# A wait of every GpSimd operation for the VectorE operation before it in the plan, in a fully planned decoder block

## The chip, the cores and the metric

The kernel runs on one core of one Trainium2 chip. The metric is device time in microseconds (us) from the start to the end of one execution; the median of several runs counts. The engines are named as in the profile: PE is TensorE (matrix products), PEld its weight loads, ACT is ScalarE, DVE is VectorE, POOL is GpSimd, SP is the engine whose queue issues the DMA transfers. SBUF is the memory that all of them read and write, PSUM the one into which TensorE writes.

## What is computed

One layer of a decoder with three parallel token mixers, for 1024 tokens of 1024 channels in float32. Cut to what matters:

```
h = rmsnorm(x);  proj = h @ w_in              # 1024 x 9744 columns
y_ssd = ssd_mixer(conv(z, xBC, dt))           # width-4 conv, chunked scan, 16 heads
y_lru = rglru_mixer(conv(lru_x), gelu gate)   # width-4 conv, linear recurrence
y_ret = retention_mixer(rotary(q, k), v, g)   # 4 heads, chunks of 128
merged = sum_k sigmoid(gate_k) * (y_k @ w_branch[k])
x = x + merged @ w_o
a, u = split(rmsnorm(x) @ ffn_w_in)           # 3072 columns each
x = x + (gelu(conv3(a)) * u) @ ffn_w_out
return rmsnorm(x)
```

## The kernel before

Activations are held transposed: channels on the 128 partitions, tokens along the row, in tiles of 128 x 512 (half of the tokens, called half 0 and 1). Every large product is done as a "quad" of two column blocks by two token halves, with seven partial products in place of eight (products named A11, S1 to S4 on the weight's side and B11, T1 to T4 on the activation's side; sums and differences of blocks are formed on VectorE at L342, L353 and L407). Each operand is split into a high part, rounded on ScalarE (L260), and a low part, the difference, formed on VectorE or GpSimd (L336 for activations, L420 for weights); three matmuls (L444 to L446) make one product. Results are combined out of PSUM on VectorE (L426). Between the quads run the small stages: convolutions (L504 to L517: a GpSimd or VectorE memset or a copy of three halo columns, one ScalarE pass and two or three VectorE steps at L514), the scan (L780 to L878), retention (L981 to L1046), the recurrence (L893 to L953), gates and sums (L1133 to L1228).

Nothing is issued directly. Every step is recorded as an `Op` in a `Plan` with the engines that may run it, an estimated duration, a priority, and its dependences. `Plan.schedule` then plays all engines against a clock and gives each Op an engine, a start and its buffers; `run` issues the Ops in the order of their planned start, with tc.manual_schedule(), so each engine's program order is the plan's. The framework places semaphore waits for the data dependences between engines, and no others.

The plan has a notion of a shared port. An Op is marked when it can run on VectorE and reads nothing from PSUM (L74):

```python
o.lock = "DVE" in engs and len({id(b) for b in r if b.tag in PSUMS}) == 0
```

and in `schedule` a GpSimd Op and a marked VectorE Op are never planned at the same time (L177, and L224 to L225):

```python
ok = not (port > t and (e == "POOL" or (e == "DVE" and o.lock))) and fits(o)
...
if e == "POOL" or (e == "DVE" and o.lock):
    port = t + dur
```

On the chip nothing holds the two engines to this: a GpSimd operation starts when its own data and buffers are there. Simple elementwise steps are recorded with `vec(..., pool=True)`, which lets the plan choose between VectorE and GpSimd; `gps` records GpSimd alone. The functions that record ScalarE and TensorE steps, and four helpers of the softplus at the start, issue their instructions inside a function that returns nothing; the others return the instruction.

Of the kernel before, what the change touches and what calls it, by code (L numbers as in the profile page):

```python
# [240 lines left out]
class K:  # L241
# [1072 lines left out]
    def run(self, gl):  # L1314
        tc, nc = self.tc, self.nc
        with tc.tile_pool(name="small", bufs=1) as small, \
                tc.tile_pool(name="big", bufs=1) as pool, \
                tc.tile_pool(name="psum", bufs=1, space=PSUM) as psum, \
                tc.tile_pool(name="dram", bufs=1, space=DRAM) as dpool:
            self.small, self.dpool = small, dpool  # L1320
            self.load_consts()
            self.record(gl)
            slots = dict(SLOTS)
            for key in self.OPS:
                for p in range(4):
                    for s in "hl":
                        slots[f"{key}{s}{p}"] = 1
            ops = self.pl.schedule(slots)
            eng = {"PE": nc.tensor, "ACT": nc.scalar, "DVE": nc.vector, "POOL": nc.gpsimd, "DMA": nc.sync}
            with tc.manual_schedule():  # L1330
                for op in ops:
                    for b in op.alloc:
                        pl = psum if b.tag in PSUMS else pool
                        b.t = pl.tile(b.shape, b.dt, name=b.name, tag=f"{b.tag}_{b.slot}")
                    op.fn(eng[op.eng])


def pairs():
# [97 lines left out]
```

## Time and profile before

| | |
|---|---|
| median of 3 runs | 2113.42 us (2112.43 to 2116.41) |
| the profiled execution | 2117.82 us, its span 2116.1 us |
| mean granted TensorE clock | 0.991 |
| busy: TensorE | 2061.2 us, 97% of the span |
| busy: VectorE | 1683.1 us, 80%, 2635 instructions |
| busy: ScalarE | 1146.4 us, 54% |
| busy: GpSimd | 652.0 us, 31%, 514 instructions |

Busy time is the time in which an instruction of the engine is under way, standing for something else included. A busy share is a mean over stages. In the timelines a row is start, duration, engine, line, operation, what it writes and reads, shape, how many such instructions are merged in the row; in brackets the idle time of the engine just before it, and what ended it. VectorE's instructions follow one another with a small overlap, so that a row may start up to 0.09 us before the one ahead of it ends.

### The profile page before, as it was taken

The page shows a single profiled execution, that of the slowest core. Times are in us where ns is not written, and L with a number is a line of the kernel's source. Part 1 is how long each engine was busy: PE and PEld are TensorE (multiplying, and loading weights), DVE is VectorE, ACT ScalarE, POOL GpSimd, SP SyncE. Part 2 cuts the span into 40 slices and gives each one's busy share as a digit, 9 for nine tenths or more (in the row PEclk, how much of TensorE's full clock was granted, in tenths as well). Part 3 has the DMA queues.
Part 4 walks back from the last instruction along what each step waited for, and adds up shares of the span by engine and source line. Part 5 has one row for each costly group of instructions (what it writes and reads, how often), then busy time and mean ns, then how long its engine had stood idle before and what let it go on. Part 6 is the DMA issues. An engine that isn't in the chain of part 4 may idle for free.

```text
span 2116.1 us, 27857 instructions
## 1 busy us (share of the span) xinstructions
PE 2061.2 (97%) x9390; PEld 1656.1 (78%) x9390; DVE 1683.1 (80%) x2635; ACT 1146.4 (54%) x1927; POOL 652.0 (31%) x514
## 2 busy tenths in 40 slices
PE   8999999999999999999999999989999999999997
PEld 4788888678888888888877877768888888887886
DVE  7979999987754557667889989897777777899887
ACT  6645465445766679999644335454434444544442
POOL 3111134432212111212466545442211221244441
PEclk9999999999999999999999999989999999999998
DMA  4333335534354544445678856713222222276764
GB/s 167 130 114 123 113 110 164 167 138 138 122 168 157 162 146 159 149 154 198 198 239 278 268 188 202 245 55 110 99 101 80 90 75 81 89 251 213 258 214 164
DMA packets 148032, 332.04 MB, mean 157 GB/s; under 512 B 16432, under 2 KB 17200, under 8 KB 147888
## 3 DMA queue, kind: packets, MB, share of 16 engines
q1 hardware_dynamic: 147888, 330.26, 47.3%
q8 instruction: 74, 1.21, 0.2%
q14 instruction: 70, 0.57, 0.1%
HBM read 235.82 MB, written 94.37 MB: 156 GB/s over the span
## 4 chain that ended last, share of the span: by engine, by line
PE 69%; DVE 6%; DMA 3%; issue 1%; ACT 1%; POOL 0%; SPq 0%; DVEq 0%; ACTq 0%; POOLq 0%
PE y_ff L444 3%; PE y_ff L446 3%; PE y_ff L445 3%; PE z_ff L446 2%; PE x_ff L445 2%; PE z_ff L444 2%; PE x_ff L444 2%; PE z_ff L445 2%; PE x_ff L446 2%; PE y_gt L446 2%; PE y_gt L444 2%; PE y_gt L445 2%; PE y_fo L444 1%; PE y_fo L446 1%; PE y_fo L445 1%; PE y_br L444 1%
## 5 line engine op out<-in xcount | busy, mean ns | idle before, releaser
L260 ACT ACT_TABLE_LOAD x102 | 130.9, 1283 | 1.9
L426 DVE TENSOR_TENSOR e_ff<-e_ff,y_ff 128x512 f32<-128x512 f32 x72 | 49.5, 687 | 60.8 <-PE y_ff L446 58.6
L1205 POOL TENSOR_TENSOR cv_fa<-cv_fa,e_ff 128x512 f32<-128x512 f32 x26 | 34.6, 1331 | 72.4 <-DVE e_ff L426 63.6
L260 ACT ACTIVATE cv_fa<-cv_fa 128x512 f32<-128x512 f32 x48 | 30.4, 633 | 44.5 <-DVE cv_fa L514 42.4
L426 DVE TENSOR_TENSOR e_gt<-e_gt,y_gt 128x512 f32<-128x512 f32 x36 | 24.6, 684 | 24.6 <-PE y_gt L446 24.6
L514 DVE SCALAR_TENSOR_TENSOR cv_fa<-o_fa,consts,cv_fa 128x512 f32<-128x512 f32 x48 | 41.3, 860 | 2.0
L1228 POOL TENSOR_TENSOR e_fo<-e_fo,xl 128x512 f32<-128x512 f32 x23 | 30.2, 1312 | 38.1 <-DVE e_fo L426 36.1
L260 ACT ACTIVATE mt<-ps_a,acs 128x128 f32<-128x128 f32 x128 | 39.1, 363 | 0.4
L514 DVE SCALAR_TENSOR_TENSOR cv_fa<-e_ff,consts,cv_fa 128x512 f32<-128x512 f32 x48 | 35.9, 748 | 1.3 <-ACT cv_fa L260 0.5
L846 POOL TENSOR_TENSOR mt<-mt,cbt 128x512 f32<-128x512 f32 x15 | 20.6, 1374 | 47.0 <-ACT mt L260 40.7
L426 DVE TENSOR_TENSOR e_ff<-e_ff,z_ff 128x512 f32<-128x512 f32 x48 | 32.9, 686 | 2.5 <-PE z_ff L446 0.9
L426 DVE TENSOR_TENSOR e_fo<-e_fo,y_fo 128x512 f32<-128x512 f32 x36 | 24.6, 684 | 9.4 <-PE y_fo L446 9.1
L514 DVE SCALAR_TENSOR_TENSOR cv_lx<-e_lx,consts,cv_lx 128x512 f32<-128x512 f32 x36 | 28.5, 821 | 0.7 <-ACT cv_lx L260 0.5
L426 DVE TENSOR_TENSOR e_br<-e_br,y_br 128x512 f32<-128x512 f32 x36 | 24.6, 683 | 5.2 <-PE y_br L446 4.9
L1139 POOL TENSOR_TENSOR e_br<-e_br,gl 128x512 f32<-128x512 f32 x17 | 23.6, 1388 | 16.6 <-DVE e_br L426 16.5
L260 ACT ACTIVATE e<-ps_a 64x512 f32<-64x512 f32 x32 | 18.9, 592 | 17.1 <-PE ps_a L834 16.9
L514 DVE SCALAR_TENSOR_TENSOR cv_xs<-e_xs,consts,cv_xs 128x512 f32<-128x512 f32 x36 | 27.7, 814 | 0.1
L925 PE MATMUL ps_l<-lxh,lwl 128*128 128x512 f32 x64 | 25.2, 394 | 0.0
L924 PE MATMUL ps_l<-lxl,lwh 128*128 128x512 f32 x64 | 25.2, 394 | 0.0
L923 PE MATMUL ps_l<-lxh,lwh 128*128 128x512 f32 x64 | 25.2, 394 | 0.0
L260 ACT ACTIVATE e_gt<-e_gt 128x512 f32<-128x512 f32 x36 | 21.8, 625 | 5.8 <-DVE e_gt L426 5.7
L868 POOL TENSOR_TENSOR xs<-xs,e 128x384 f32<-128x384 f32 (+1 forms) x10 | 13.3, 1330 | 35.1 <-DVE xs L866 28.4
(6116 smaller groups left out, 8059.4 us busy)
## 6 DMA issues: line engine op xcount, KB each, us to landing
wr_ff<-in_ffn_in_dram SPq DMA_DIRECT2D x50, 512.0 KB, 3.8
wr_fo<-in_ffn_out_dram SPq DMA_DIRECT2D x43, 512.0 KB, 4.4
wr_br<-in_w_branch_dram SPq DMA_DIRECT2D x35, 512.0 KB, 4.7
yl<-yd SPq DMA_DIRECT2D x60, 256.0 KB, 4.9
gl<-g SPq DMA_DIRECT2D x60, 256.0 KB, 4.5
wr_gt<-in_w_quads_dram SPq DMA_DIRECT2D x24, 512.0 KB, 5.0
gl<-gt SPq DMA_DIRECT2D x48, 256.0 KB, 3.7
g<-cv_fa SPq DMA_DIRECT2D x48, 256.0 KB, 2.0
```

The source lines that it names most:

```text
L260: e.activation(out(), in_(), func, **kw)
L426: q.k.vec(lambda e: e.tensor_tensor(out.t[:, O:], a.t[:, O:], ps.t, ALU.add), [a, ps], [out], prio=pr)
L444: e.matmul(ps.t, ah.t[:, c], bh.t, start=(start and m == 0), stop=False, **kw)
L445: e.matmul(ps.t, ah.t[:, c], bl.t, start=False, stop=False, **kw)
L446: e.matmul(ps.t, al.t[:, c], bh.t, start=False, stop=(m == 3), **kw)
L514: self.vec(lambda e, s=s: e.scalar_tensor_tensor(cv.t[:, O:], raw.t[:, O - s : W - s], w(taps - 1 - s), cv.t[:, O:], ALU.mult, ALU.add), [ ...
L923: e.matmul(p_.t, wh.t[:, s], h.t, start=(k == 0), stop=False)
L924: e.matmul(p_.t, wh.t[:, s], l.t, start=False, stop=False)
L925: e.matmul(p_.t, wl.t[:, s], h.t, start=False, stop=(k == 1))
L1139: self.vec(lambda e: e.tensor_tensor(out.t[:, o], ap(), g.t[:, o], ALU.mult), [buf, g], [out], pool=not ps)
L1205: self.vec(lambda e: e.tensor_tensor(a.t[:, o], a.t[:, o], u.t[:, o], ALU.mult), [a, u], [a], pool=True)
L1228: self.vec(lambda e: e.tensor_tensor(out.t[:, o], ap(), x.t[:, o], ALU.add), [buf, x], [out], pool=not ps)
```

## The change

The loop that issues the plan remembers the last VectorE instruction that came from a marked Op (`op.lock`) and returned an instruction. Each GpSimd instruction then gets a dependence on it, of the class that is kept by a semaphore, so that it does not start before that VectorE instruction has ended. The plan itself, its order, engines and buffers are as before.

```diff
             eng = {"PE": nc.tensor, "ACT": nc.scalar, "DVE": nc.vector, "POOL": nc.gpsimd, "DMA": nc.sync}
+
+            info = mybir.DependencyInfo(mybir.DependencyClass.Sync, mybir.DependencyReason.DATA)
+            holder = None
             with tc.manual_schedule():
                 for op in ops:
                     for b in op.alloc:
                         pl = psum if b.tag in PSUMS else pool
                         b.t = pl.tile(b.shape, b.dt, name=b.name, tag=f"{b.tag}_{b.slot}")
-                    op.fn(eng[op.eng])
+                    ins = op.fn(eng[op.eng])
+                    if op.eng == "DVE" and op.lock and ins is not None:
+                        holder = ins
+                    elif op.eng == "POOL" and holder is not None:
+                        tc.add_manual_dep(ins.ins, holder.ins.name, info, reason="port order")
```

## Rows read from the trace of the kernel before

**Rows 1.** The page of the profile: the engines' busy time, share and instructions, and the chain of work that ended last, its share by engine.

```profile
span 2116.1 us, 27857 instructions
...
PE 2061.2 (97%) x9390; PEld 1656.1 (78%) x9390; DVE 1683.1 (80%) x2635; ACT 1146.4 (54%) x1927; POOL 652.0 (31%) x514
...
PE 69%; DVE 6%; DMA 3%; issue 1%; ACT 1%; POOL 0%; SPq 0%; DVEq 0%; ACTq 0%; POOLq 0%
```

**Rows 2.** The view of waits, TensorE's alone: who waited for whom, us in total, times, the longest.

```profile
PE ss_fin L551 <- DVE acc_fin L571: 2.6, 1, 2.6
...
PE x_ff L445 <- POOL h2B11l L336: 1.2, 1, 1.2
...
PE ps_y L862 <- POOL mt L846: 0.6, 1, 0.6
```

**Rows 3.** The timeline around 1395 us, VectorE's and GpSimd's rows; ahead of them one unhindered row of each, at 1390 and 1391.

```profile
1390.14 0.69 DVE L342 TENSOR_TENSOR h2T<-e_wo,x 128x512 f32<-128x512 f32 x1
...
1394.48 1.29 DVE L342 TENSOR_TENSOR h2T<-e_wo,x 128x512 f32<-128x512 f32 x1
...
1395.69 1.77 DVE L342 TENSOR_TENSOR h2T<-e_wo,x 128x512 f32<-128x512 f32 x1
...
1391.45 1.28 POOL L420 TENSOR_TENSOR ff0A22l<-wr_ff,ff0A22h 128x512 fp32r<-128x512 f32 x1 [1.78 <-ACT ff0A22h L260]
...
1395.16 1.74 POOL L336 TENSOR_TENSOR h2T2l<-x,h2T2h 128x512 fp32r<-128x512 f32 x1
```

**Rows 4.** The timelines of GpSimd and VectorE: two memsets, the VectorE operation in whose time the second falls, and the step that reads its columns.

```profile
115.19 0.10 POOL L508 MEMSET o_B<- 128x3 f32 x1
...
1490.26 1.23 DVE L510 COPY e_ff<-halo 128x3 f32<-128x3 f32 x1
...
1491.37 0.10 POOL L508 MEMSET o_fa<- 128x3 f32 x1
...
1501.32 0.76 DVE L514 SCALAR_TENSOR_TENSOR cv_fa<-o_fa,consts,cv_fa 128x512 f32<-128x512 f32 x1
```

**Rows 5.** The timeline of GpSimd: the first and the last of 57 GpSimd operations with inputs that start while the VectorE operation before them in the plan runs.

```profile
42.48 1.87 POOL L336 TENSOR_TENSOR hB22l<-x,hB22h 128x512 fp32r<-128x512 f32 x1 [1.62 <-ACT hB22h L260]
...
2027.27 1.68 POOL L1228 TENSOR_TENSOR e_fo<-e_fo,xl 128x512 f32<-128x512 f32 x1 [1.23 <-DVE e_fo L426]
```

**Rows 6.** The chain of work that ended last, in order of time: start, us, what (POOLq is GpSimd's sequencer), near 1369, 1146 and 1401 us.

```profile
1369.34 0.60 DVE acc_ffn L571
...
1370.06 0.02 POOLq L1166
1370.08 1.26 POOL acc_ffn L571
...
1146.73 4.50 DMA yl<-yd
...
1401.17 0.67 DVE cv_fa L514
```

**Rows 7.** The timelines: VectorE operations that stood behind a GpSimd operation which had itself stood behind the VectorE operation before; the first (381) and the last (2024) of ten, two between, and a GpSimd row that follows the one at 1938.

```profile
381.76 1.78 DVE L1309 TENSOR_TENSOR e_qk<-e_qk,rt 128x512 f32<-128x512 f32 x1
...
389.41 1.68 DVE L846 TENSOR_TENSOR mt<-mt,cbt 128x512 f32<-128x512 f32 x1
...
1938.01 1.79 DVE L342 TENSOR_TENSOR g1T<-gl,gl 128x512 f32<-128x512 f32 x1
...
1945.16 1.74 POOL L336 TENSOR_TENSOR g1B22l<-gl,g1B22h 128x512 fp32r<-128x512 f32 x1
...
2024.81 1.79 DVE L342 TENSOR_TENSOR g2T<-gl,gl 128x512 f32<-128x512 f32 x1
```

**Rows 8.** The timelines: VectorE operations that started after a GpSimd operation which the plan has behind them; of 12, the GpSimd operation of the first (138), both operations of the last (1298), and three of VectorE's between.

```profile
138.29 1.30 POOL L420 TENSOR_TENSOR xs0A11l<-wr_xs,xs0A11h 128x512 fp32r<-128x512 f32 x1 [2.88 <-ACT xs0A11h L260]
...
438.06 1.77 DVE L407 TENSOR_TENSOR v1S<-wr_v 128x512 f32<-128x512 f32 x1
...
1141.61 1.82 DVE L342 TENSOR_TENSOR y2T<-yl,yl 128x512 f32<-128x512 f32 x1
...
1143.35 1.79 DVE L342 TENSOR_TENSOR y2T<-yl,yl 128x512 f32<-128x512 f32 x1
...
1298.24 1.75 POOL L336 TENSOR_TENSOR mgT2l<-m,mgT2h 128x512 fp32r<-128x512 f32 x1
...
1298.76 1.79 DVE L407 TENSOR_TENSOR wo0S<-wr_wo,wr_wo 128x512 f32<-128x512 f32 x1
```

**Rows 9.** The timeline of TensorE: five matmuls before which it stood, the stop in brackets.

```profile
385.95 1.16 PE L851 MATMUL ps_of<-Cm,sv 128*128 128x128 f32 x8 [1.39 <-DVE sv L825]
...
444.68 0.50 PE L444 MATMUL x_v<-hB21h,v0A12h 128*128 128x512 f32 x1 [0.80 <-ACT e_v L260]
...
1156.39 0.50 PE L444 MATMUL y_br<-y2T3h,br20S3h 128*128 128x512 f32 x1 [1.68 <-DVE e_br L426]
...
1405.03 0.51 PE L444 MATMUL z_ff<-h2T1h,ff1S1h 128*128 128x512 f32 x1 [1.20 <-ACT ff1S1h L260]
...
1950.30 0.50 PE L444 MATMUL x_fo<-g1B21h,fo11A12h 128*128 128x512 f32 x1 [2.92 <-ACT e_fo L260]
```

**Rows 10.** The timelines of GpSimd and TensorE: a GpSimd operation that starts inside a VectorE operation, and the matmuls that read its result.

```profile
331.10 1.56 POOL L846 TENSOR_TENSOR mt<-mt,cbt 128x512 f32<-128x512 f32 x1 [6.38 <-ACT mt L260]
...
332.71 0.98 PE L862 MATMUL ps_y<-mt,xdt 128*64 128x128 f32 x13 [0.65 <-POOL mt L846]
```

## The prediction

> **What bounds the kernel now.** I read the page first, for which engine is full; then TensorE's waits, for what stops that engine; then the two timelines of VectorE and GpSimd side by side, because the change touches only the order between those two; last the chain of waits, to see which of their operations lie ahead of a TensorE stop. The reader is to see that TensorE is busy for 2061.2 of the 2116.1 us span, with most of the chain that ended last on it, 6% on VectorE and 0% on GpSimd, which is busy 31% of the time [rows 1]. So no change in the order of VectorE and GpSimd can give more than the 54.9 us in which TensorE stands idle, and of those some are the first load and waits for ScalarE. The longest single wait that VectorE ends is 2.6 us, and only two waits are GpSimd's own, 1.2 and 0.6 us [rows 2].
>
> **What the two engines do to each other.** An h2T subtraction of two SBUF tiles takes 0.69 us when nothing is in its way. The one at 1395.69 takes 1.77, because the GpSimd operation that started at 1395.16 sits in the middle of it; and that GpSimd operation, issued 0.61 us before the VectorE operation ahead of it ended, takes 1.74 where an unhindered one takes 1.28 to 1.30 [rows 3]. So one of the two runs and the other stands still, and both durations grow by the time of standing. Who comes first decides which one pays.
>
> **The change part by part.** It adds a wait to GpSimd operations and nothing else: no work moves, no queue is reordered, VectorE waits for nothing new. Behind the waiting GpSimd operation only later GpSimd operations are queued; for them wait the DMA stores of their results, VectorE operations that read them, and TensorE where the result is a low half of a split operand.
>
> I laid the program's order over the trace: engine by engine the instructions of the trace come in that order, so every GpSimd operation of the plan has a known VectorE predecessor with all operands in SBUF (the holder). There are 510 of them. Of these 148 wait already, by a semaphore of their own or of an earlier GpSimd operation, for that holder or a later VectorE operation; 362 get a wait that is new. In 418 of the 510 the holder had ended when the GpSimd operation started, and the wait is met. What is left is 92 operations in three kinds.
>
> (a) 23 memsets of three columns. They start inside the holder, from o_B at 115.19 to the o_fa ones of the FFN, and take 0.10 us like any other [rows 4]. They would start 0.2 to 0.7 us later (18 of them 0.2 to 0.3: the holder's last 0.12 us and the wake-up). The convolution step that reads the columns of the one at 1491.37 starts at 1501.32 [rows 4]; under that cover I price this at nothing, and with the cover gone at 0.25 us for each of the 18.
>
> (b) 57 two-input operations that start while the holder runs, from hB22l at 42.48 to e_fo at 2027.27 [rows 5]. Today they stand until the holder ends and finish about 1.13 us after it (1395.16 + 1.74 less 1395.77, where the first h2T of that place ends [rows 3]). With the wait they start after the semaphore: the trace has 0.14 us from the end of a VectorE operation (1369.34 + 0.60) to the start of a GpSimd operation that waits for it (1370.08), with sequencer steps between [rows 6]; and then 1.28 us. That is 0.29 later; where fewer steps lie between it is a little less, and I take 0.25: 57 x 0.25 = 14 us of GpSimd time, on an engine that is idle for two thirds. A VectorE operation that now stands behind such an operation stands as much longer; about 20 do, 5 us of VectorE time.
> In 14 of the 57, though, the next VectorE operation also reads two SBUF tiles and follows at once. Now GpSimd, already in line, goes ahead of it; with the wait GpSimd is not yet in line and VectorE goes first. In ten of these VectorE stood about 1.08 us (1.78 less 0.69), the first at 381.76 and the last at 2024.81 [rows 7]: 10.7 us of VectorE time come back.
>
> (c) 12 operations that started up to half a us before their holder, from 138.29 to 1298.24 [rows 8]. The plan has the holder first; on the chip it came second and stood some 1.0 us each, 12.3 us together. All of this comes back, and the 12 GpSimd operations end about 1 us later.
>
> Extra sequencer steps: I count at most 163 more on GpSimd, a few hundredths of a us each [rows 6]; cover is its idle time. So VectorE gains 23.0 and loses 5, of 1683.1 us.
>
> **What of it reaches TensorE.** Only what lies ahead of a TensorE stop, and no more than the stop:
>
> 1. 381.76 and 389.41 (1.09 and 0.99): the stop at 385.95, 1.39 us, for sv, which follows the first on VectorE. I take 1.1.
> 2. 438.06 (1.08) is on the chain; the stop at 444.68 is 0.80 us and named to ScalarE, so 0.5.
> 3. 1141.61 and 1143.35 (1.13 and 1.10): the chain goes from there over m to a load of yl, 4.50 us, and back to VectorE, up to the stop of 1.68 at 1156.39. A load and ScalarE lie between and may not move by the whole; I take 1.0.
> 4. 1395.69 (1.08): the chain runs on over VectorE to the conv step at 1401.17, before the stop of 1.20 at 1405.03. I take 1.0.
> 5. 1938.01 (1.10): a stop of 2.92 at 1950.30, but between them, as at 1945.16, GpSimd and VectorE stand for each other in the planned order, which the change leaves. I take 0.7.
>
> These are [rows 3, 6 to 9]. Together 4.3 us. What I take off: the mt product at 331.10 stands already (1.56 us), and TensorE waits for it 0.65 us; it will be 0.25 us later at least, 0.9 if another VectorE operation slips ahead [rows 10]. And the 5 us that VectorE loses under (b), at the share in which gains arrive (4.3 of 23.0), are 0.9. Sum: -4.3 + 0.25 + 0.9 = -3.15, and I take -3.
>
> The profiled span is 2116.1 us (2117.8 as a run), 4.4 above the median of the runs shown, 2113.42; the sum is a difference, so I put it on the median: **2110.4 us**.
>
> Bounds. Every stop above filled to its own size or the stall's: 1.39 + 0.80 + 1.68 + 1.08 + 1.10 = 6.05, and the five other stalls of (b) and nine of (c) might add 2 by the same share (some 15 us times 0.19 is 2.9, less what I count off): 2105. The other way, none of the gain arrives, the 1.15 us of losses stay, and three GpSimd operations lose one more turn of 0.8 us each (0.69 and a wake-up) on the way to TensorE: 2113.4 + 3.6 = 2117.0.
>
> A row against a rule: the standing GpSimd operation ends 1.13 us after the VectorE operation before it, an unhindered one takes 1.28 to 1.30 us, so part of its start-up is done while it stands, and the wait throws that part away [rows 3]. The Trainium skill, SBUF — State Buffer, section "SBUF: two separate sides", has it that the ports the two engines share are locked for the whole instruction by whoever starts first, and the other fully blocks. By that rule alone a wait in place of standing costs only the wake-up and the sum would be -4.3 in place of -3.15; this lies between my forecast and the first rival.
>
> **The rivals.**
>
> - Gains arrive in full. For it: the stalls in front of places 1 to 4 are as large as the stops, or nearly. Against: what is late next is a load (place 3), ScalarE (2, 4) or GpSimd itself (5). Time: 2113.4 - 6 = 2107.4.
> - Nothing moves. For it: 418 of 510 waits are met, and TensorE stands only 2.6% of the span. Against: stalls of 1.1 us on the chain are plain rows. Time: 2113.
> - Slower: GpSimd loses its turn. Place: the operand splits and qk rotations, where VectorE issues two-input operations back to back. A GpSimd operation that wakes 0.1 us after its holder finds the port taken again and gives up 0.69 us, and the next is queued behind it. I count about 20 of the 57 with a reader less than 1 us behind their end; mt has TensorE 0.05 us behind [rows 10]. Price: 0.25 to 1.05 us each; if all of them pass it on, 20 x 0.25 = 5 and more. It decides from the point at which more than five operations lose a whole turn with their reader on TensorE's way. Against it: GpSimd ends 0% of the chain [rows 1] and only two TensorE waits. Time: 2113.4 + 5 = 2118.4.
>
> **How the numbers follow.** A measurement of this kernel can tell about 0.2%, 4.2 us, from no change. My forecast (a gain of 1 to 4 us, unmeasurable) 0.48; gains in full, beyond 4.2 us, 0.31; nothing moves 0.11; slower 0.10. So faster 0.31, same 0.59, slower 0.10. The range of 2105.0 to 2117.0 takes in forecast, nothing and nearly all of the gains in full, and leaves out the slower rival and what lies beyond the bounds.
>
> **What would show it.** In the changed profile the h2T subtraction near 1395 and the two y2T near 1141 take 0.69 us, and GpSimd starts about 0.1 us or more after its holder ends; few GpSimd operations near 1.74 us are left. VectorE's busy time falls by 15 to 23 us; GpSimd's falls by some 25, since standing under (b) turns into idle time. TensorE's stops at 385.95, 1156.39 and 1405.03 shrink, the one at 332.71 grows. If VectorE's busy time falls and TensorE's stops do not, the gain went to a load or ScalarE; if new waits of TensorE for GpSimd appear, the slower rival holds; if VectorE's busy time stays, the waits did not do what I read from the listing.

## The result, and the profile after

The changed kernel takes 2103.22 us (median of four runs, 2101.64 to 2104.5), the kernel before beside it 2114.07 (four runs, 2112.43 to 2116.41): a ratio of 0.9947, 95% interval 0.993 to 0.9965. A second measurement, with five runs, gave 0.9944 (0.993 to 0.9957). The gain is 11 us; forecast were 3, and the time lies below the range, whose low end was 2105.0.

The page of the changed kernel (to be held against [rows 1]), with the first lines of its parts 1 and 4:

```profile
span 2102.7 us, 27972 instructions
...
PE 2056.5 (98%) x9390; PEld 1654.1 (79%) x9390; DVE 1656.9 (79%) x2635; ACT 1146.9 (55%) x1927; POOL 613.4 (29%) x514
...
PE 70%; DVE 4%; DMA 3%; ACT 1%; issue 1%; POOL 1%; SPq 0%; DVEq 0%; ACTq 0%; POOLq 0%
```

Two subtractions say where the 13.4 us between the two spans went. TensorE's idle time is the span less its busy time: 54.9 us before, 46.2 after, 8.7 less. Its busy time fell as well, by 4.7 us, over the same 9390 matmuls. The prediction had a term for the first and none for the second. (The profiled run of before was its kernel's longest, so these two differences are on the large side: in profiles of three kernels below, whose ratios to before are 0.9994 to 1.0011, TensorE idles 50.5, 50.9 and 53.7 us and is busy 2060.5 to 2061.2.) VectorE is busy 26.2 us less, GpSimd 38.6 us less.

VectorE and GpSimd near the place of [rows 3], which the changed kernel reaches ten us earlier; x2 is two operations in a row:

```profile
1385.50 1.29 DVE L342 TENSOR_TENSOR h2T<-e_wo,x 128x512 f32<-128x512 f32 x2
...
1383.09 1.29 POOL L420 TENSOR_TENSOR ff0A22l<-wr_ff,ff0A22h 128x512 fp32r<-128x512 f32 x1
...
1386.94 2.55 POOL L336 TENSOR_TENSOR h2T2l<-x,h2T2h 128x512 fp32r<-128x512 f32 x2 [1.32 <-ACT h2T1h L260]
```

Two h2T subtractions in 1.29 us, where one alone took 1.77: neither stands. The h2T2l operation, which had come in the middle of them, comes after them, and takes 1.28 in place of 1.74. Counted over the whole timeline, 99 two-input GpSimd operations took over 1.4 us before, and 5 do now; of VectorE's, 125 took over 1 us, and 97 do now.

TensorE at four of the five stops of [rows 9] and at the one of [rows 10]:

```profile
332.43 1.09 PE L862 MATMUL ps_y<-mt,xdt 128*64 128x128 f32 x14 [0.93 <-POOL mt L846]
...
383.72 1.16 PE L851 MATMUL ps_of<-Cm,sv 128*128 128x128 f32 x8 [0.30 <-DVE sv L825]
...
1149.33 0.51 PE L444 MATMUL y_br<-y2T3h,br20S3h 128*128 128x512 f32 x1 [0.91 <-DVE e_br L426]
...
1394.60 0.50 PE L444 MATMUL z_ff<-h2T1h,ff1S1h 128*128 128x512 f32 x1 [0.89 <-ACT ff1S1h L260]
...
1936.71 0.39 PE L444 MATMUL x_fo<-g1B21h,fo11A12h 128*128 128x512 f32 x1
```

The matmuls run in the same order in both kernels, so the difference of two start times is the lead gained up to there: 2.23 us at ps_of (385.95 less 383.72), 7.06 at y_br, 10.43 at z_ff, 13.59 at x_fo. At x_fo the stop, 2.92 us before, is gone; at ps_y it grew from 0.65 to 0.93, as the prediction had it.

Between 676 and 681 us the lead also grows from 2.6 to 4.7 us, but not through the change. VectorE and TensorE there in the profile of before:

```profile
673.98 3.48 DVE L1046 TENSOR_TENSOR ry<-ry,sg 128x512 f32<-128x512 f32 x2
...
679.87 0.66 PE L1001 MATMUL ps_vt<-consts,v 128*128 128x128 f32 x4 [1.37 <-ACT ktm L260]
```

VectorE in a kernel with one wait alone, which is not at this place ("One place alone" below):

```profile
670.95 1.28 DVE L1046 TENSOR_TENSOR ry<-ry,sg 128x512 f32<-128x512 f32 x2
```

Two ry products took 3.48 us in that one execution of before, both standing. In all thirteen other profiles, with a wait at this place or without one, they take 1.3 and the stop of 1.37 us behind them is gone. Five of the kernels below (those with 484, 445, 41, four waits and one) have none on the two GpSimd operations there, numbers 147 and 148, and their lead grows by 2.0 us here as well. So 2.0 of the 13.4 us between the two spans belong to the profiled execution and not to the change.

One sign of the prediction came true by half. Of the two y2T near 1141 [rows 8] the second takes 0.69 us now, but the first still stands and takes 1.79, behind a y2B22l that the plan has ahead of it (VectorE and GpSimd in the changed kernel):

```profile
1136.33 2.39 DVE L342 TENSOR_TENSOR y2T<-yl,yl 128x512 f32<-128x512 f32 x2
...
1134.56 3.00 POOL L336 TENSOR_TENSOR y2B22l<-yl,y2B22h 128x512 fp32r<-128x512 f32 x2 [0.69 <-DVE m L1143]
```

### The profile page after: what moved, and what is told of

It is laid out like the page before. It is cut to its first block, busy times and chain, and to the rows that moved or that the text cites. A ratio compares the mean times of both kernels' runs of the same rounds, so it can differ in the third digit from the quotient of the medians.

```text
span 2102.7 us, 27972 instructions
## 1 busy us (share of the span) xinstructions
PE 2056.5 (98%) x9390; PEld 1654.1 (79%) x9390; DVE 1656.9 (79%) x2635; ACT 1146.9 (55%) x1927; POOL 613.4 (29%) x514
## 4 chain that ended last, share of the span: by engine, by line
PE 70%; DVE 4%; DMA 3%; ACT 1%; issue 1%; POOL 1%; SPq 0%; DVEq 0%; ACTq 0%; POOLq 0%
PE y_ff L444 3%; PE y_ff L446 3%; PE y_ff L445 3%; PE x_ff L445 2%; PE x_ff L444 2%; PE x_ff L446 2%; PE z_ff L446 2%; PE z_ff L444 2%; PE z_ff L445 2%; PE y_gt L446 2%; PE y_gt L444 2%; PE y_gt L445 2%; PE y_fo L444 1%; PE y_br L444 1%; PE y_fo L446 1%; PE y_fo L445 1%
## 5 line engine op out<-in xcount | busy, mean ns | idle before, releaser
L846 POOL TENSOR_TENSOR mt<-mt,cbt 128x512 f32<-128x512 f32 x15 | 19.3, 1290 | 39.9 <-DVE cv_lx L514 16.9
```

## The experiments

Each kernel is measured beside the kernel before, on the same chip. GpSimd's waits are numbered in the order in which the change adds them. TensorE's idle time (span less busy) and VectorE's busy time are from one profile each, and vary by some us.

| kernel | ratio to before, 95% interval | TensorE idle / busy | VectorE busy |
|---|---|---|---|
| before | 1 | 54.9 / 2061.2 | 1683.1 |
| changed | 0.9947 (0.993 to 0.9965) | 46.2 / 2056.5 | 1656.9 |
| changed, again | 0.9944 (0.993 to 0.9957) | 45.5 / 2055.0 | 1659.1 |
| the prediction's 26 waits | 0.9974 (0.9965 to 0.9983) | 51.0 / 2057.0 | 1671.7 |
| the other 484 | 0.9976 (0.9966 to 0.9987) | 47.0 / 2057.9 | 1672.9 |
| 510 waits, three holders back | 1.0011 (1.0002 to 1.002) | 50.5 / 2060.5 | 1685.6 |
| one wait, g1T2l's | 0.9994 (0.9985 to 1.0003) | 50.9 / 2061.2 | 1685.5 |
| the 65 turned round | 0.9942 (0.9929 to 0.9954) | 42.7 / 2056.8 | 1647.3 |
| the other 445 | 1.0001 (0.9992 to 1.001) | 53.7 / 2061.2 | 1687.6 |
| four waits, g1B22l's | 0.999 (0.9981 to 0.9999) | 51.5 / 2060.0 | 1679.9 |
| waits on any VectorE operation | 1.0099 (1.0082 to 1.0116) | 65.8 / 2074.5 | 1698.5 |
| 158 moved behind VectorE | 1.0081 (1.0068 to 1.0095) | 64.1 / 2064.6 | 1640.6 |
| 256 moved behind VectorE | 1.0294 (1.028 to 1.0308) | 92.5 / 2083.7 | 1648.3 |
| 41 of the 65, unlisted | 0.9951 (0.9937 to 0.9965) | 45.4 / 2057.6 | 1665.2 |

**The prediction's own places.** The waits on the operations that the prediction counted as giving VectorE the first turn (14 under (b), 12 under (c)), and in a second kernel all the others (`not in`):

```diff
+            npool = -1
+            SWAPS = [8, 25, 32, 36, 42, 88, 89, 103, 104, 136, 137, 147, 148, 157, 165, 179, 190, 207, 238, 243, 244, 293, 302, 337, 461, 490]
...
-                        tc.add_manual_dep(ins.ins, holder.ins.name, info, reason="port order")
+                        npool += 1
+                        if npool in SWAPS:
+                            tc.add_manual_dep(ins.ins, holder.ins.name, info, reason="port order")
```

> Only 26 of the 510 waits: those of the 12 GpSimd operations that started before their holder and of the 14 that were in line for the port ahead of a VectorE operation which followed at once. Theory (the waits gain by letting VectorE go first where the order was in fact turned round): nearly the whole gain of the change, 8 to 11 us below the kernel before, near 2104; VectorE's busy time falls by about 23 us. Rival 1 (every wait gains a little, since a GpSimd operation that starts later disturbs VectorE less): 26/510 of the gain, under 1 us. Rival 2 (the gain is in the 43 operations with inputs that merely stood behind a running holder): no gain.

> The other 484 waits, without those 26. Theory: no gain or a small loss, 2113 to 2116, since here only the wake-up of GpSimd is added and no VectorE operation goes earlier; GpSimd's busy time still falls by about 20 us as standing turns into waiting. Rival 1: nearly the whole gain, 9 to 11 us. Rival 2: the whole gain.

The 26 gave 0.26%, 5.5 us: somewhat more than the prediction's 4.3, less than the 8 to 11 expected of them here. The other 484, which the prediction priced at a loss of 1.15 us, gave 0.24%, 5.1 us: half of the gain lies where it saw none. TensorE at the five matmuls of [rows 9], with the 26 alone:

```profile
382.86 1.16 PE L851 MATMUL ps_of<-Cm,sv 128*128 128x128 f32 x8 [0.30 <-DVE sv L825]
...
440.69 0.39 PE L444 MATMUL x_v<-hB21h,v0A12h 128*128 128x512 f32 x1
...
1150.31 0.50 PE L444 MATMUL y_br<-y2T3h,br20S3h 128*128 128x512 f32 x1 [1.51 <-DVE e_br L426]
...
1396.83 0.50 PE L444 MATMUL z_ff<-h2T1h,ff1S1h 128*128 128x512 f32 x1 [0.81 <-ACT ff1S1h L260]
...
1941.53 0.50 PE L444 MATMUL x_fo<-g1B21h,fo11A12h 128*128 128x512 f32 x1 [2.53 <-ACT e_fo L260]
```

The five stops shrink by 1.1, 0.8, 0.2, 0.4 and 0.4 us, 2.8 in all.

**The waits without their order.** Each GpSimd operation waits for the VectorE operation three holders earlier, so there are as many added dependences, and in the trace of before 470 of the 510 are met:

```diff
-                        holder = ins
+                        held.append(ins)
+                        holder = held[-4] if len(held) > 3 else None
```

> Every GpSimd operation waits, but for the marked VectorE operation three before its holder: new waits of the same kind on most of the operations, which are met when the operation comes. Theory: within 1.5 us of the kernel before, 2113 to 2115.5, VectorE's busy time unchanged. Rival 3 (the gain is not the order at the port but something that the waits bring with them, other waits that fall away or an order of release of buffers): most of the gain, 6 us or more.

1.0011: waits that don't keep the planned order bring nothing and cost at most 0.2%. The comparison is not quite even: this program holds 27911 instructions, 54 more than before, the changed one 115 more, since a wait that another one implies is not issued.

**One place alone.** Only wait 461, that of g1T2l before the g1T at 1938.01 [rows 7]; the edit is that of the 26 with `npool == 461`.

> One wait of the 510: that of the GpSimd operation g1T2l at 1937.50 us, which stood behind e_fo and then went ahead of the subtraction g1T. Theory: VectorE's g1T falls from 1.79 to 0.69 us, the stop of TensorE at 1950.30 (2.92 us) falls by 1 us or more, and with it may go the 3.4 us at half the granted clock behind that stop (1.7 us); together 1 to 4.7 us, 2109.5 to 2113. The lead of the changed kernel grows by 4.0 us at this stop, which another 0.8 follows in the half-clock stretch. Rivals 1 and 3: nothing measurable.

0.9994, and the stop at x_fo shrank only to 2.53. The timeline shows why. GpSimd and VectorE before, behind the place that the prediction looked at:

```profile
1942.27 1.77 DVE L420 TENSOR_TENSOR fo13A11l<-wr_fo,fo13A11h 128x512 fp32r<-128x512 f32 x1
1943.97 1.78 DVE L336 TENSOR_TENSOR g1T2l<-gl,g1T2h 128x512 fp32r<-128x512 f32 x1
1945.67 3.46 DVE L342 TENSOR_TENSOR g1T<-gl,gl 128x512 f32<-128x512 f32 x2
...
1941.74 6.83 POOL L336 TENSOR_TENSOR g1B22l<-gl,g1B22h 128x512 fp32r<-128x512 f32 x4
```

GpSimd with the one wait, and in the changed kernel:

```profile
1936.56 6.83 POOL L336 TENSOR_TENSOR g1B22l<-gl,g1B22h 128x512 fp32r<-128x512 f32 x4
```

```profile
1934.00 1.30 POOL L336 TENSOR_TENSOR g1B22l<-gl,g1B22h 128x512 fp32r<-128x512 f32 x1 [3.11 <-ACT g1T3h L260]
...
1936.13 1.28 POOL L336 TENSOR_TENSOR g1B22l<-gl,g1B22h 128x512 fp32r<-128x512 f32 x1 [0.83 <-DVE fo13A12l L420]
...
1940.64 2.54 POOL L336 TENSOR_TENSOR g1B22l<-gl,g1B22h 128x512 fp32r<-128x512 f32 x2 [3.22 <-ACT fo10S1h L260]
```

Before, four g1B22l run without a break, and each makes one VectorE operation stand (four of them in 7.0 us, 2.8 unhindered). With the one wait they still do. In the changed kernel they are spread over nine us, each behind its holder. So these four were turned round, and the prediction had said of this place that GpSimd and VectorE stand for each other "in the planned order, which the change leaves".

**The planned order.** This leads back to how the holder was found. The order of the plan is the list that the planner returns, `sorted(ops, key=lambda o: (o.start, o.idx))` (L234), and the change takes the holder from it. The prediction took it from the listing of the compiled program, which has each engine's instructions in the plan's order but merges the engines in another: it names another VectorE operation for 115 of the 510, in 114 of them an earlier one. With the plan's own order laid over the trace of before, 358 waits are met (not 418), 58 operations with inputs start inside the holder, and 65 (not 12) start before their holder does; of 29 memsets whose wait is not met, 28 start before the holder too. Then the waits of these 65 alone, and all but these; the edit is that of the 26 with `in TURNED` and `not in TURNED`:

```diff
+            TURNED = [8, 12, 36, 42, 44, 51, 55, 62, 87, 88, 89, 103, 104, 106, 132, 136, 137, 140, 147, 148, 155, 157, 165, 179, 190, 202, 203, 204, 207, 209, 213, 217, 218, 238, 243, 244, 246, 248, 249, 251, 253, 293, 298, 302, 303, 304, 305, 319, 327, 333, 336, 337, 338, 442, 443, 461, 463, 464, 465, 466, 490, 491, 492, 493, 494]
```

> Only the waits of 65 GpSimd operations: those that, in the kernel before, started ahead of their holder when the holder is taken from the order in which the plan issues (in the first set of 26 it was taken from the order of the listed program, in which I had found 12 such operations). Theory, mended (the gain comes from every place where the plan's order was turned round at the port, and there are 65, not 12): 8 to 11 us below the kernel before, 2103 to 2106; VectorE's busy time falls by 22 us or more. Rival 1 (every wait gains a little): 65/510 of the gain, 1.4 us.

> The other 445 waits, without those 65: 58 operations that start while their holder runs, 29 memsets, and 358 whose wait is met. Mended theory: within 2 us of the kernel before, 2112 to 2116, VectorE's busy time within 5 us of before. Rival 1: 9 us or more below it. Rival 2 (what merely stood behind a running holder is the gain): 5 us or more below it.

The page's line on the engines, of the 65 and of the 445:

```profile
PE 2056.8 (98%) x9390; PEld 1654.4 (79%) x9390; DVE 1647.3 (78%) x2635; ACT 1147.1 (55%) x1927; POOL 633.3 (30%) x514
```

```profile
PE 2061.2 (97%) x9390; PEld 1655.9 (78%) x9390; DVE 1687.6 (80%) x2635; ACT 1146.5 (54%) x1927; POOL 634.3 (30%) x514
```

The 65 have the whole gain (0.9942), the 445 none (1.0001). VectorE's busy time falls by 35.8 us with the first and rises by 4.5 with the second (by 2.0 against the 1685.5 and 1685.6 of two kernels that gain nothing); GpSimd's falls by about 18 with each, so a shorter GpSimd time is no sign of a gain.

**The unlisted ones.** 24 of the prediction's 26 are among the 65. The 41 that it did not have, alone; the edit is that of the 65 with these 41 numbers in the list:

```diff
+            TURNED = [12, 44, 51, 55, 62, 87, 106, 132, 140, 155, 202, 203, 204, 209, 213, 217, 218, 246, 248, 249, 251, 253, 298, 303, 304, 305, 319, 327, 333, 336, 338, 442, 443, 463, 464, 465, 466, 491, 492, 493, 494]
```

> The change's wait on 41 GpSimd operations alone: those of the 65 that, by the order of the plan, started before their holder, which the prediction did not have among its places (it read the holder from the listing of the compiled program). The kernel with the wait on all 65 has a ratio of 0.9942 to the kernel before, the one with the prediction's 26 has 0.9974 [0.9965, 0.9983]. Theory (the gain is that of the turned-round operations, and the prediction missed most of them): 0.996 to 0.9975, some 5 to 8 us, with VectorE's busy time 15 to 25 us below 1683.1. Rival (the gain is in the prediction's places, and the two halves only help each other): 0.999 or above.

0.9951, 10.4 us: more than theory gave them, and nearly all of what the 65 bring. With the 5.5 us of the 26 that is 16, against 12.3 together, so the two halves overlap. TensorE's waits at three stops that the prediction did not list, or left in part, first before and then with the 41:

```profile
PE x_ff L444 <- ACT h2B11h L260: 3.3, 1, 3.3
...
PE x_fo L444 <- ACT e_fo L260: 2.9, 1, 2.9
...
PE ps_a L834 <- ACT mt L260: 1.1, 1, 1.1
```

```profile
PE x_ff L444 <- ACT h2B11h L260: 2.1, 1, 2.1
...
PE x_fo L444 <- ACT e_fo L260: 0.4, 1, 0.4
...
PE ps_a L834 <- ACT mt L260: 0.3, 1, 0.3
```

The stops of ps_of and z_ff, too, fall to 0.3 and 0.9 with the 41, much as with the 26 (0.30 and 0.81): there either half is enough, which is part of the overlap. One result does not fit: the other 484 contain these 41 and gave only 5.1 us (the two intervals just miss each other). So the 443 waits that the two kernels differ by took back some 5 us there, while beside the 65 they cost nothing that can be seen (0.9947 and 0.9944 against 0.9942). No run here tells why.

**Four g1B22l alone** (waits 463 to 466; the edit is that of the 26 with these numbers):

> Four waits of the 510: those of the four g1B22l operations between 1941.74 and 1948.57, which ran ahead of fo13A11l, g1T2l and two g1T on VectorE although the plan has them behind. Mended theory: these four VectorE operations take 0.68 each in place of 1.76 to 1.78, VectorE is some 4 us earlier there, the stop of TensorE at 1950.30 (2.92 us) falls by 2 us or more, and the 3.4 us at half the granted clock behind it go: 2 to 4 us below the kernel before, 2111 to 2113. If only the stop moves and not the clock: 2 to 3 us. Rivals: nothing measurable.

The stop of 2.92 us vanishes. The lead grows by 3.1 us at x_fo and by 1.7 more in the six us behind it; by 1977 us 2.0 of it are given back, and the ratio is 0.999, some 2 us.

TensorE's clock is part of it. The windows view in stretches of four to ten us (after the window: PE, PEld, DVE, ACT, POOL busy, granted clock, DMA share, GB/s), first before, then changed:

```profile
1224.00:1228.00 4.00, 3.56 (x9) 2.84 (x10) 3.87 (x7) 2.09 (x4) 1.66 (x1) 0.57 0.65 214
1371.00:1381.00 10.00, 7.93 (x22) 6.26 (x23) 8.26 (x14) 5.90 (x11) 10.00 (x9) 0.50 0.36 105
...
1391.00:1398.00 7.00, 6.18 (x15) 4.58 (x16) 7.00 (x10) 4.74 (x9) 6.55 (x5) 0.53 0.27 95
...
1951.00:1955.00 4.00, 4.00 (x13) 3.08 (x12) 2.97 (x6) 1.19 (x2) 0.00 (x0) 0.57 0.78 243
```

```profile
1364.00:1374.00 10.00, 9.20 (x29) 7.87 (x30) 5.90 (x11) 4.12 (x9) 8.37 (x8) 0.50 0.19 68
...
1384.00:1388.00 4.00, 3.77 (x10) 2.76 (x10) 3.87 (x7) 3.20 (x7) 2.68 (x3) 0.57 0.39 134
...
1938.00:1942.00 4.00, 4.00 (x18) 2.96 (x17) 3.40 (x6) 1.69 (x3) 1.36 (x2) 1.00 1.05 399
```

A granted clock of 0.50 is the lower of the two levels, 1.2 GHz. Before, TensorE worked at it at four places, about the ends of its stops near 1225, 1371, 1390 and 1950 us; in the changed kernel at two of these (the start of the kernel and its last 12 us, alike in both, are left out). With (1 less the clock) times the length, the windows of before lose 1.7 + 5.0 + 3.3 + 1.7 = 11.7 us, those of the changed kernel 5.0 + 1.7 = 6.7. The 5.0 between them is what TensorE's busy time fell by (4.7).

The other profiles agree in sum. Between 22 and 2085 us the stretches at the lower clock add up to 20.5 to 23.9 us in the five kernels of the table whose TensorE is busy for 2060.0 to 2061.2 us, and to 13.7 to 17.1 in the six with 2055.0 to 2057.9: half of the difference is 1.7 to 5.1 us. Where they fall is another matter. With the 445 waits the stop at x_fo is as long as before, and the clock behind it stays up (TensorE's row, and the windows view):

```profile
1949.18 0.50 PE L444 MATMUL x_fo<-g1B21h,fo11A12h 128*128 128x512 f32 x1 [2.98 <-ACT e_fo L260]
```

```profile
1950.00:1954.00 4.00, 4.00 (x19) 3.27 (x18) 4.00 (x8) 1.79 (x3) 0.00 (x0) 1.00 0.87 268
```

So a single stretch, such as the one behind x_fo, can't be put down to the stop ahead of it alone.

**A stricter order.** Each GpSimd operation waits for the VectorE operation before it in the plan, those that read PSUM included:

```diff
-                    if op.eng == "DVE" and op.lock and ins is not None:
+                    if op.eng == "DVE" and ins is not None:
```

> Every GpSimd operation waits for the VectorE operation before it in the plan whatever that one reads, PSUM too. Theory: operations that read PSUM do not stand for GpSimd, so the added waits buy nothing, GpSimd starts later by up to one operation of VectorE (0.69 us) and at times by a VectorE wait for TensorE; within 3 us of the changed kernel, 2102 to 2106, rather above. Rival 4 (GpSimd kept to the plan's order is what gains, port or not): 2 us or more below the changed kernel, 2101 or less.

1% slower, where at most 3 us on the changed kernel were expected. Two of TensorE's waits that name GpSimd:

```profile
PE ps_y L862 <- POOL mt L846: 2.9, 4, 1.5
...
PE x_ff L445 <- POOL h2B11l L336: 2.2, 1, 2.2
```

In the changed kernel they are 0.9 and 1.5, and all waits that name GpSimd come to 2.4 us, here to 6.7. So the prediction's slower rival is at work, with more waits than the change adds, but it is the smaller part of the 33 us between the two kernels: TensorE's busy time alone is 18.0 us longer.

**VectorE first at more places.** If a standing VectorE operation is what costs, then 97 are left. In the changed kernel the planned order is altered: a GpSimd operation that nothing up to the next VectorE operation with all operands in SBUF depends on is issued behind that one, if it is planned to start by the GpSimd operation's end; in the first kernel only where its first reader is planned 1.5 us or more after its planned end, in the second anywhere (j is that VectorE operation's place in the list, None where something depends on p before it):

```diff
+            while i < len(ops):
+                p = ops[i]
+                if p.eng == "POOL":
...
+                    if j is not None and min((o.start for o in p.succ), default=1e9) > p.end + 1.5:
+                        ops[i : j + 1] = ops[i + 1 : j + 1] + [p]
```

> The change's kernel, with 158 of the GpSimd operations issued behind the next VectorE operation with all operands in SBUF instead of in front of it (nothing between the two depends on them, and their first reader is planned at least 1.5 us after their planned end). Theory (what costs is a VectorE operation that stands behind a GpSimd operation; the change lets VectorE go first at the 65 places at which the plan already has it first): 97 of VectorE's two-tensor operations still take over 1 us in the changed kernel; at these 158 places they would fall to about 0.68 us, VectorE's busy time would go from 1656.9 to 1600 to 1630 us, and the time would be 2 to 5 us below the changed kernel's, 2098 to 2101 us (0.992 to 0.993 of the kernel before). Rival (GpSimd's results now come too late, each by the VectorE operation that it waits for): VectorE's busy time falls as well, but TensorE's waits for GpSimd grow, and the time is that of the changed kernel or above it (0.995 or more).

> As the run before it, but without the condition on the first reader: 256 GpSimd operations are issued behind the next VectorE operation with all operands in SBUF. Theory: VectorE's busy time falls furthest (below that of the run with 158), but some of the 98 added ones have a reader close behind, so TensorE's waits for GpSimd rise; the time is above that of the run with 158, between 2099 and 2112 us. Rival (only VectorE's standing counts, GpSimd has slack everywhere): the time falls below that of the run with 158, by about 98/158 of what that one gains on the changed kernel.

> The changed kernel once more, unaltered, beside the two others on the same chip. Theory and rival alike: 0.993 to 0.9965 of the kernel before, as measured; its profile gives a second reading of TensorE's stops (36.5 us in the first) and of the time at the lower granted clock (38 us before the last matmul in the first). By the theory the place at 1930 to 1950 us again shows no stop over 1 us before the first matmul that reads g1B22l, against 2.92 us in the kernel before.

The changed kernel, measured once more beside these two, gives 0.9944, and again the first x_fo matmul that reads g1B21h and fo11A12h has no stop before it. The theory fell: 1.0081 and 1.0294, both slower than the kernel before, though VectorE's busy time is below the changed kernel's in both (1640.6 and 1648.3; 1600 to 1630 was expected of the first). With 158 moved, VectorE and GpSimd near 1886 us, and TensorE a little later:

```profile
1886.61 1.79 DVE L342 TENSOR_TENSOR g0T<-gl,gl 128x512 f32<-128x512 f32 x1
...
1886.23 1.61 POOL L336 TENSOR_TENSOR g0B22l<-gl,g0B22h 128x512 fp32r<-128x512 f32 x1 [3.53 <-PE z_fo L445]
...
1892.04 0.74 PE L444 MATMUL y_fo<-g0T3h,fo00S3h 128*128 128x512 f32 x1 [1.20 <-DVE e_fo L426]
```

In the changed kernel this g0B22l ran ahead of the VectorE operations, and the same stop is 0.19 us. Moved behind one of them, it starts inside the next and makes the one after stand: 76 GpSimd operations take over 1.4 us (5 in the changed kernel), and 103 of VectorE's over 1 us (97). So moving an operation by one place moved the collision, and its result came later. The rival's reason doesn't hold for the 158: TensorE's waits that name GpSimd come to 3.3 us (2.4 in the changed kernel), those that name VectorE to 26.0 (19.1) and ScalarE to 19.3 (8.7). With 256 moved, TensorE also waits for GpSimd's own results: mt 6.7 us, lxl 3.4, xds 2.4 in its waits. VectorE's busy time alone is thus no measure of the gain; at this place it mattered which operation stood ahead of a TensorE stop.

## Why the prediction was wrong

- **The failing step** is "so every GpSimd operation of the plan has a known VectorE predecessor": the predecessor was read off a listing that does not keep the plan's order between engines. From it came the counts of 418 met and 12 under (c), where the plan gives 358 and 65; the gain sits in the 65 and not in the others (0.9942 against 1.0001), and most of it in the 41 that were missed (0.9951).
- **Place 5** fell with it: forecast 0.7 us; the lead grew by 3.1 us at x_fo and by 1.7 behind it, where before worked at the lower clock, and 1.7 were given back by 1977.
- **What of it reaches TensorE.** Its own 26 were given too much at the places: forecast were 1.1, 0.5, 1.0, 1.0 and 0.7, and with these waits alone the stops shrank by 1.1, 0.8, 0.2, 0.4 and 0.4. Place 3 gave least, and there the first y2T still stands (1.80 us in that kernel). That the 26 came out near in sum, 5.5 us against 4.3, is luck: 2.8 us are the five stops, and TensorE's busy time is 3.5 to 4.2 us below that of before and of the three kernels that gain nothing, a term that the sum did not have.
- **A missing term.** No price stood for TensorE's clock; TensorE's busy time fell by 4.7 us, which is more than the whole forecast.
- **The losses** were priced at 1.15 us. The 445 waits in which they lie changed nothing that can be seen (1.0001, interval 0.9992 to 1.001, so from 1.7 us gained to 2.1 lost). VectorE lost 2.0 to 4.5 us there, of 5 expected. Some 5 us were lost beside the 41, and none beside the 65, so a price for them stays open. The Trainium skill, SBUF — State Buffer, section "SBUF: two separate sides", states the exclusive lock from which the prediction worked out a sum of -4.3. The 445 do not contradict it; 1.15 us is too little to tell the two sums apart here.
- **The memsets** were given a delay of 0.2 to 0.7 us, by the same wrong holder. The one at 1491.37 comes 4.4 us later in the changed kernel, since its holder by the plan is a later VectorE operation:

```profile
1485.38 0.10 POOL L508 MEMSET o_fa<- 128x3 f32 x1 [4.39 <-DVE cv_fa L1205]
```

Its reader starts at 1490.88 there, so the price of nothing held.

- **Right** were the mechanism (VectorE's stall at 1395 and one of the two at 1141 gone, GpSimd waiting and no longer standing), the stop at ps_y that grew to 0.93, and that the slower rival needs far more lost turns. VectorE's busy time fell by 26.2 us, forecast 15 to 23; GpSimd's by 38.6, forecast 25.
- **The low bound** of 2105 was made of the five listed stops filled to their size, so it could hold no stop that the list had missed. The rival "gains in full" (2107.4, chance 0.31) had the right sign and the same fault.
- **Still open**: why the lead gained at one place is given back in part a few us on (0.7 to 1.8 us at four places; at one of them a stop for xds grew from 0.13 to 1.16 us), and why the other waits cost some 5 us beside the 41 and nothing beside the 65.

## What to carry to other kernels

Where an edit refers to what precedes an operation in a plan, take the precedence from the list that issues the operations, not from a listing in which the engines' streams are merged anew; then lay it over the trace and count the pairs that ran the other way round. A queue that runs ahead of its plan can cost the fuller engine time although it ends hardly a wait itself (1.8 us of TensorE's here), and 65 waits that only restore the planned order gave 0.58% back; waiting for every VectorE operation, or a new order, cost 0.8 to 2.9%. In a sum on TensorE's stops leave room for matmuls at the lower granted clock as well. And before a difference of two profiles is put down to a change, look for it in profiles of kernels without that part of the change: here 2.0 us of it belonged to one execution.

## What the runs showed of the hardware

- In the kernel before, TensorE worked at the lower clock for 3.4 to 10 us behind stops in an otherwise busy stretch: the matmul at 1951.43, 4.0 us after TensorE had stopped and 1.1 after it had started again, takes 0.63 us where its like take 0.39 to 0.40. The clock need not fall there: behind the same stop, 2.98 us long, it stayed at 1.00 with the 445 waits, and in the changed kernel it stayed at 1.00 after TensorE had been busy for 2.33 of the four us from 1214; before it fell to 0.50 at the same work, after 2.25 of the four us from 1220.
- 510 more dependences of GpSimd, of which 470 are met in the trace of before, cost 0.02 to 0.2% (1.0011).
- With the 445 waits GpSimd's busy time is 18 us shorter and the time is where it was, 1.0001: GpSimd operations whose records grow by standing are not a cost by that alone.
- In one execution of before two VectorE products stood for 1.1 us each behind GpSimd operations near 674 us, and in thirteen executions of other kernels neither did: without a wait, which of the two engines comes first can differ from one execution to the next.
